# Two stages of a two-layer block: fewer whole key tiles, maxima earlier and a scaling on another engine in the second attention; transposes of gathered rows in halves between the expert products

## The chip, the cores and the metric

The kernel is one launch on one core of a Trainium2 chip. The metric is the device time of that launch in microseconds (us); 4358.14 us is the median of three runs of the kernel before. The engines named here are TensorE (PE; PEld is its weight load), VectorE (DVE), ScalarE (ACT), GpSimd (POOL) and SyncE (SP, which issues most DMAs).

## The reference

Two transformer-like blocks run one after the other on 2048 rows of 1024 features, in float32. The first mixes latent attention and a state space model; it is not touched. The second block, cut to what matters:

```
qa, ka, va, qr, kr, vr, gr = split(hx @ w_in)          # 8 query heads, 2 key heads of 64
k = concat([ka_context, ka]); v = concat([va_context, va])   # 256 + 2048 = 2304 keys
attn = softmax(q @ k.T * 64**-0.5) @ v                 # bidirectional, every query sees every key
ret  = group_norm(retention(qr, kr, vr)) * gn_g + gn_b # 4 heads of 128: (o - mean) * rsqrt(var + eps)
x2 = x + gt1 * (concat([attn, ret * silu(gr)]) @ w_out)
h2 = modulate(rms_norm(x2))
# experts: one group of 4, then 2 of its 8 experts; 32 experts, each 1024 -> 512 -> 1024
y[token] += weight * ((silu(h2 @ w_gate[e]) * (h2 @ w_up[e])) @ w_down[e])
out = rms_norm(x2 + gt2 * y)
```

## The kernel before

Precision: most products are three fp32r products of split operands (`mm3`, L306: high by high, high by low, low by high). A split is a cast on ScalarE (`split`, L318) and a subtraction on VectorE (L319). A product with float32 operands takes two passes of the tensor engine, which the trace shows as two MATMUL records.

**Order.** The functions are Python code that traces instructions in program order. A planner then makes, when the program is built, one fixed list for each engine: when an engine is free in its plan, it takes from the instructions whose inputs and buffers are ready in the plan the one that stands first in program order. On the chip each engine goes through its list in order, and waits where an input or a buffer is later than planned. Tiles come from pools; a tag has a number of buffers (`bufs`), and a new tile of that tag waits until the oldest one's last reader is done.

**Second attention (`Attention2`, from L1097).** Sixteen blocks of 128 queries by two key heads make 32 units. In a unit, `run` (L1265) goes over 18 key tiles, t = 0 to 17, of 128 keys. For each t: `scores` makes two fp32r products (L1185, L1186) into a PSUM tile `ps`; `exps` takes the exponential on ScalarE (L1194, or L1192); five tiles behind, `values` multiplies the exponentials with the values. There are two kinds of key tile. For a *whole* tile (`WHOLE2`, L1093: 2, 4, 7, 9, 12, 14, 17) the exponential stays float32 and one float32 product is made (L1228, two passes; the ones in its weights give the sum of the exponentials). For a *split* tile the exponential is cast to a high part `ph` (L1196, ScalarE), the rest `pl` is subtracted on VectorE (`rest`, L1205), the high part is added to a sum `acc` on GpSimd (L1212), and two fp32r products are made (L1232, L1233).

While unit n runs, `top` (L1157) finds the maxima that unit n + 1 subtracts: twenty steps of a product `pa` (L1167, two PSUM buffers) and a maximum over its columns on VectorE (`nm`, L1168), one step for the maximum `mx` over these (L1171), and one step with four transposes of `mx` and the copy of its negative into `qm` on ScalarE (L1176). `TOP` (L1107) says how many of these 22 steps are called after key tile t; what is left is done at t = 0 of the next unit, before its first scores, whose second product needs `qm`.

At t = 1, 9, 11 and 15 (`SIDE`) one step of the retention is called (`Retention.steps`). Its second loop has six steps for each of 16 chunks: transposes of queries and keys; transposes of scaled queries and the next state `rst` (L1049); scores; output `on` copied to SBUF with its mean and variance (L1070, L1072) and the inverse root `r4` (L70 on VectorE, then a power on GpSimd, L72); the scaling of `on` on VectorE, one instruction for each of four heads (L1076); and transposes of `on` with the group norm's gain on ScalarE (`ot`, L1084). The transposes here and those of `mx` share one PSUM buffer.

**Experts (`phase_moe`, L2345).** 32 experts in order of their row counts. The 15 largest have two blocks of 128 rows, the others one (a loop at the end takes what is left over); `turns` (L2075) sets them in turn, one of one block, one of two. For each expert three weight matrices of 2 MB come in four chunks each; each chunk is split into `whi` (ScalarE, L2250) and `wlo` (VectorE, or GpSimd for every sixth, L2253). There are 5 buffers for raw chunks and 12 for split ones, so the splits run about a matrix or two ahead of the products.

`rows` (L2258) gathers 128 rows of `h2` by an indirect DMA on GpSimd's queue into `xg` (two buffers), and transposes them in two halves of four 128 x 128 transposes into a PSUM tile `pt` (two buffers), each split into `xh` and `xl`. `gate` and `up` (through `into`, L2274) multiply in four chunks of six matmuls for each block of rows. `turned` (L2303) transposes the hidden tile `hg` through the same two `pt` buffers and splits it into `hh` and `hl`. `down` (L2316) gathers the rows of `x2` into `xo`, makes two products `py` of twelve matmuls for each block, scales, adds, normalizes and scatters the rows back.

One turn of the loop (L2372) has this program order, for the expert at hand (xs), the next one (xs2) and the one after (xs3): shares of xs2; gate weights and gate of xs2; `turned` of xs; up weights and up of xs2; `begin` of xs3, which reads its number on SP, gathers its rows, transposes and splits all of them; down weights and down of xs.

Of the kernel before, what the change touches and what calls it, by code (L numbers as in the profile page):

```python
# [10 lines left out]
F = mybir.dt.float32  # L11
# [869 lines left out]
HR = 4  # L881
# [71 lines left out]
class Retention:  # L953
# [16 lines left out]
    def steps(self, wk, bank):  # L970
# [55 lines left out]
        for n in range(NT):  # L1026
# [46 lines left out]
            k.rsqrt(r4, mv[:, :, 1], 1)  # L1073
            yield
            for h in range(HR):
                nc.vector.tensor_scalar(on[:, h], on[:, h], mv[:, h, 0:1], r4[:, h:h + 1], op0=OP.subtract, op1=OP.mult)  # L1076
# [16 lines left out]
WHOLE2 = (2, 4, 7, 9, 12, 14, 17)  # L1093
# [3 lines left out]
class Attention2:  # L1097
# [7 lines left out]
    TOP = (1, 1, 1, 2, 1, 1, 2, 1, 2, 1, 1, 1, 1, 1, 1, 1, 1, 1)  # L1105
# [1121 lines left out]
class Experts:  # L2227
# [30 lines left out]
    def rows(self, tx, lx):  # L2258

        k, nc, wk = self.k, self.k.nc, self.wk  # L2260
        xg = wk.tile([128, D], F, name="xg")
        nc.gpsimd.indirect_dma_start(out=xg, out_offset=None, in_=k.h2,
                                     in_offset=bass.IndirectOffsetOnAxis(ap=tx, axis=0))
        xh, xl = (wk.tile([128, 8, 128], R, name="x" + n, bufs=self.xs) for n in "hl")
        for half in range(2):
            pt = self.ps.tile([128, 4, 128], F, name="pt")
            for q in range(4):
                k.tr(pt[:, q], xg[:, (4 * half + q) * 128:(4 * half + q + 1) * 128])
            split(nc, xh[:, 4 * half:4 * half + 4], xl[:, 4 * half:4 * half + 4], pt)
        return tx, lx, xh, xl  # L2270

    def into(self, name, xs, w):
# [17 lines left out]
    def up(self, xs, hs, w):  # L2290
        for hg, z in zip(hs, self.into("pu", xs, w)):
            self.k.nc.vector.tensor_tensor(hg, hg, z, op=OP.mult)
# [23 lines left out]
    def down(self, xs, ts, w, gt, tbs):  # L2316
# [28 lines left out]
def phase_moe(k):  # L2345
# [6 lines left out]
    with ExitStack() as ctx:  # L2352
        x = Experts(k, ctx, 5, 12, 4, 3)

        def begin(r):
            e = nc.sync.value_load(k.ids[0:1, r:r + 1], min_val=0, max_val=NE - 1)
            return e, [x.rows(k.txs[:, b, r:r + 1], k.lxs[:, b, r:r + 1]) for b in range(2 if r < N2 else 1)]
# [4 lines left out]
        e, xs = begin(seq[0])  # L2362
# [7 lines left out]
        with k.tc.issue_after(x.mm.ins):  # L2370
            e2, xs2 = begin(seq[1])
# [16 lines left out]
def phase_end(k):  # L2388

    nc = k.nc  # L2390
    with ExitStack() as ctx:
# [3 lines left out]
        with k.tc.For_i(0, n, 1) as i:  # L2395
# [24 lines left out]
            rows = [x.rows(*places(k, wk, ix))]  # L2420
# [64 lines left out]
```

## Time and profile before

| | |
|---|---|
| runs | 4355.51, 4358.14 (median), 4358.15 us |
| profiled execution | 4347.35 us, span of its instructions 4345.5 us |
| granted clock, mean over the span | 0.961 |
| TensorE, VectorE busy over the span | 4035.4 us (93%), 2956.5 us (68%) |
| ScalarE, GpSimd busy over the span | 2153.2 us (50%), 1766.6 us (41%) |
| second attention | 2111 to 3079 us |
| experts | from about 3355 us to the end |

Busy times are sums over the whole span; the two stages have their own. A matmul's record is longer than the time it keeps the engine, since matmuls overlap: the distance from one start to the next tells what it costs. In rows of the order of time, the bracket is the idle time of the engine before the instruction and what ended it. The granted clock is the share of TensorE's full clock that was granted; its two levels are 1.2 and 2.4 GHz.

### The profile page before, as it was taken

The numbers are of one execution on the slowest core, as the hardware profiler recorded it, in microseconds if no ns is written. First come the engines' busy times: TensorE is split into PE (matmuls) and PEld (weight loads), VectorE is DVE, ScalarE is ACT, GpSimd is POOL, SyncE is SP. The second block draws the span as 40 slices with busy tenths as digits, with TensorE's granted clock in tenths as the row PEclk, the third lists the DMA queues.
The fourth block names the chain that finished last, engine by engine and source line by source line (L and its number), as shares of the span: only waits on it lengthen the run. The fifth ranks groups of instructions, "written<-read, shape, count | busy, mean of one in ns | idle before, by whom it ended". The sixth has DMA issues, their size and how long they took to land. (4 is left out here: it accounts for less than half of the span.)

```text
span 4345.5 us, 59078 instructions
## 1 busy us (share of the span) xinstructions
PE 4035.4 (93%) x19522; PEld 3202.2 (74%) x19522; DVE 2956.5 (68%) x5239; ACT 2153.2 (50%) x3910; POOL 1766.6 (41%) x2209
## 2 busy tenths in 40 slices
PE   7999879999998899999999999999997899999996
PEld 5777768888886778788666666666686677777775
DVE  7564258888644447544588788777565788888885
ACT  3233355555543334332366666666421666665664
POOL 3340058885001532222365555555200444444442
PEclk9999989999999999999999999999998999999998
DMA  5543772232225445333531211211533788887884
GB/s 141 164 152 119 232 240 75 92 104 81 69 75 171 137 148 183 119 117 102 145 111 53 60 47 51 56 38 33 154 133 118 284 285 292 289 285 279 278 283 155
DMA packets 436483, 646.66 MB, mean 149 GB/s; under 512 B 92193, under 2 KB 232737, under 8 KB 435917
## 3 DMA queue, kind: packets, MB, share of 16 engines
q1 hardware_dynamic: 407356, 561.75, 40.5%
q0 software_dynamic: 21840, 66.25, 4.1%
q10 hardware_dynamic: 6976, 14.85, 1.1%
q8 instruction: 155, 2.54, 0.2%
q14 instruction: 156, 1.27, 0.1%
HBM read 495.88 MB, written 155.64 MB: 150 GB/s over the span
## 5 line engine op out<-in xcount | busy, mean ns | idle before, releaser
L2253 DVE TENSOR_TENSOR wlo<-raw,whi 128x1024 fp32r<-128x1024 f32 x320 | 500.8, 1578 | 60.6 <-ACT whi L2250 55.0
L1168 DVE TENSOR_REDUCE nm<-pa 128x1 f32<-128x512 f32 (+1 forms) x640 | 391.7, 630 | 134.3 <-PE pa L1167 131.1
L2250 ACT CAST whi<-raw 128x1024 fp32r<-128x1024 f32 x384 | 387.2, 1051 | 147.1 <-PE pu L310 61.1
L1212 POOL TENSOR_TENSOR acc<-acc,ph 128x512 f32<-128x512 f32 x288 | 368.8, 1281 | 192.3 <-ACT ph L1196 187.6
L1167 PE MATMUL pa<-kk,q 128*128 128x512 f32 (+1 forms) x640 | 307.9, 490 | 28.6 <-DVE nm L1168 22.8
L310 PE MATMUL z<-wh,hlo 128*128 128x512 f32 (+2 forms) x816 | 305.7, 375 | 0.0
L308 PE MATMUL z<-wh,hhi 128*128 128x512 f32 (+2 forms) x768 | 291.2, 381 | 6.5 <-DVE zo L455 2.4
L1194 ACT ACTIVATE ps<-ps 128x512 f32<-128x512 f32 x352 | 204.5, 586 | 179.6 <-PE ps L1186 149.0
L309 PE MATMUL z<-wl,hhi 128*128 128x512 f32 (+2 forms) x768 | 290.2, 378 | 2.5 <-DVE wl L319 2.5
L1205 DVE TENSOR_TENSOR pl<-ps,ph 128x512 fp32r<-128x512 f32 x352 | 238.5, 683 | 43.9 <-ACT ph L1196 40.8
L72 POOL TENSOR_TENSOR nr<-nr,mhalf 128x1 f32<-128x1 f32 x98 | 61.3, 627 | 500.7 <-DVE nr L70 440.9
L1185 PE MATMUL ps<-q,kk 128*128 128x512 f32 x576 | 250.5, 435 | 0.1
L661 PE MATMUL s<-kn,q 128*128 128x512 f32 x768 | 229.8, 407 | 9.3 <-ACT p L674 5.5
L1186 PE MATMUL ps<-qm,kl 65*128 65x512 f32 x576 | 233.6, 407 | 0.2 <-ACT qm L1176 0.2
L1228 PE MATMUL o<-p,vw 128*128 128x512 f32 x448 | 229.1, 592 | 0.0
L693 ACT CAST ph<-pt 128x512 fp32r<-128x512 f32 x256 | 143.0, 597 | 152.1 <-PE pt L65 148.9
L739 PE MATMUL o<-ph,v 128*128 128x256 f32 x1024 | 215.6, 292 | 0.2 <-ACT ph L693 0.2
L697 DVE TENSOR_TENSOR pl<-pt,ph 128x512 fp32r<-128x512 f32 x256 | 168.0, 685 | 67.1 <-ACT ph L693 66.5
L1196 ACT CAST ph<-ps 128x512 fp32r<-128x512 f32 x352 | 202.7, 589 | 17.3 <-ACT ps L1194 0.4
L1167 PEld LDWEIGHTS pa<-kk,q 128*128 128x128 f32 x640 | 124.2, 194 | 110.8 <-DVE nm L1168 58.4
L2253 POOL TENSOR_TENSOR wlo<-raw,whi 128x1024 fp32r<-128x1024 f32 x64 | 159.8, 2496 | 95.6 <-ACT whi L2250 94.3
L661 PEld LDWEIGHTS s<-kn,q 128*128 128x128 f32 x768 | 141.5, 191 | 53.8 <-ACT p L674 6.4
(631 smaller groups left out, 11685.6 us busy)
## 6 DMA issues: line engine op xcount, KB each, us to landing
raw<-in_moe_w_gate SPq DMA_DIRECT2D x128, 512.0 KB
raw<-in_moe_w_up SPq DMA_DIRECT2D x128, 512.0 KB
raw<-in_moe_w_down SPq DMA_DIRECT2D x128, 512.0 KB
raw<-in_w_in SPq DMA_DIRECT2D x136, 256.0 KB
w<-in_w_ada SPq DMA_DIRECT2D x96, 256.0 KB
xt<-in_x SPq DMA_DIRECT2D x32, 512.0 KB
xt<-x SPq DMA_DIRECT2D x28, 512.0 KB
rv<-rv SPq DMA_DIRECT2D x34, 256.0 KB
```

Of the source, the lines that this page charges most:

```text
L308: nc.tensor.matmul(out, lh, rh, start=start, stop=False)
L309: nc.tensor.matmul(out, lh, rl, start=False, stop=False)
L310: return nc.tensor.matmul(out, ll, rh, start=False, stop=stop)
L661: self.nc.tensor.matmul(sp[:, c - c0:e - c0], l, r, start=n == 0, stop=n == len(ops) - 1)
L1167: nc.tensor.matmul(pa[:, :c1 - c0], q[:, h], kk[:, c0:c1], start=True, stop=True)
L1168: nc.vector.tensor_reduce(nm[:, h, c:c + 1], pa[:, :c1 - c0], axis=AX.X, op=OP.max)
L1185: nc.tensor.matmul(ps, kk[:, ts], q, start=True, stop=False)
L1186: nc.tensor.matmul(ps, kl[:, ts], qm, start=False, stop=True)
L1205: nc.vector.tensor_tensor(lo, ps, hi.bitcast(F), op=OP.subtract)
L1212: nc.gpsimd.tensor_tensor(acc, u["acc"], hi.bitcast(F), op=OP.add)
L2250: nc.scalar.copy(hi, raw)
L2253: i = eng.tensor_tensor(lo, raw, hi.bitcast(F), op=OP.subtract)
```

## The change

In the second attention: (1) four key tiles are whole, 3, 8, 13 and 17, where there were seven; the other fourteen are split. (2) `TOP` has other counts. (3) The scaling of `on` by mean and inverse root is an activation on ScalarE with scale `r4` and bias `m4`, where `m4` = -mean * r4 is made by one new VectorE instruction for all four heads, in the same step as the root.

```diff
             k.rsqrt(r4, mv[:, :, 1], 1)
+            m4 = wk.tile([128, HR], F, name="m4")
+            nc.vector.scalar_tensor_tensor(m4, mv[:, :, 0], -1.0, r4, op0=OP.mult, op1=OP.mult)
             yield
             for h in range(HR):
-                nc.vector.tensor_scalar(on[:, h], on[:, h], mv[:, h, 0:1], r4[:, h:h + 1], op0=OP.subtract, op1=OP.mult)
+                nc.scalar.activation(on[:, h], on[:, h], AF.Identity, scale=r4[:, h:h + 1], bias=m4[:, h:h + 1])
...
-WHOLE2 = (2, 4, 7, 9, 12, 14, 17)
+WHOLE2 = (3, 8, 13, 17)
...
-    TOP = (1, 1, 1, 2, 1, 1, 2, 1, 2, 1, 1, 1, 1, 1, 1, 1, 1, 1)
+    TOP = (1, 2, 1, 2, 1, 1, 2, 1, 1, 2, 1, 1, 2, 1, 1, 1, 0, 1)
```

In the experts: `rows` takes all blocks of an expert, issues their gathers, and returns a generator of steps; a step is one half of one block (four transposes and the split), in the order first half of each block, then second half of each. `begin` of xs3 stands ahead of `turned`. `up` of xs2 takes a step before its chunks 1 and 3, `down` of xs one after each of its products `py`, and what is left is done after `down`. So four steps of a two-block expert lie two in up and two in down, and the two steps of a one-block expert both in up. The first two experts and the loop at the end do all steps at once.

```diff
-    def rows(self, tx, lx):
+    def rows(self, ixs):
         k, nc, wk = self.k, self.k.nc, self.wk
-        xg = wk.tile([128, D], F, name="xg")
-        nc.gpsimd.indirect_dma_start(out=xg, out_offset=None, in_=k.h2,
-                                     in_offset=bass.IndirectOffsetOnAxis(ap=tx, axis=0))
-        xh, xl = (wk.tile([128, 8, 128], R, name="x" + n, bufs=self.xs) for n in "hl")
-        for half in range(2):
-            pt = self.ps.tile([128, 4, 128], F, name="pt")
-            for q in range(4):
-                k.tr(pt[:, q], xg[:, (4 * half + q) * 128:(4 * half + q + 1) * 128])
-            split(nc, xh[:, 4 * half:4 * half + 4], xl[:, 4 * half:4 * half + 4], pt)
-        return tx, lx, xh, xl
+        xs, gs = [], []
+        for tx, lx in ixs:
+            gs.append(wk.tile([128, D], F, name="xg"))
+            nc.gpsimd.indirect_dma_start(out=gs[-1], out_offset=None, in_=k.h2,
+                                         in_offset=bass.IndirectOffsetOnAxis(ap=tx, axis=0))
+            xs.append((tx, lx, *(wk.tile([128, 8, 128], R, name="x" + n, bufs=self.xs) for n in "hl")))
+
+        def steps():
+            for h in (slice(0, 4), slice(4, 8)):
+                for xg, (_, _, xh, xl) in zip(gs, xs):
+                    pt = self.ps.tile([128, 4, 128], F, name="pt")
+                    for q in range(4):
+                        k.tr(pt[:, q], xg[:, (h.start + q) * 128:(h.start + q + 1) * 128])
+                    split(nc, xh[:, h], xl[:, h], pt)
+                    yield
+        return xs, steps()
...
         for c in range(4):
+            if c % 2:
+                next(steps, None)
...
                     mm3(nc, py, hh[:, q], hl[:, q], w[q][0][:, ns], w[q][1][:, ns], q == 0, q == 3)
+                next(steps, None)
...
+            steps = iter(())
+            if n + 1 < NE:
+                e3, xs3, steps = begin(seq[n + 1])
             ts = x.turned(hs)
             if n < NE:
-                x.up(xs2, hs2, x.weights(e2, 1))
-            if n + 1 < NE:
-                e3, xs3 = begin(seq[n + 1])
-            x.down(xs, ts, x.weights(e, 2), k.gt2, tbs)
+                x.up(xs2, hs2, x.weights(e2, 1), steps)
+            x.down(xs, ts, x.weights(e, 2), k.gt2, tbs, steps)
+            for _ in steps:
+                pass
```

## Rows read from the trace of the kernel before

**Rows 1.** Busy us (instructions) by engine, granted clock, DMA share, GB/s by stage.
```profile
core 0: us, PE busy (x) PEld busy (x) DVE busy (x) ACT busy (x) POOL busy (x), PEclk, DMA share, GB/s
2703.20:2729.00 25.80, 25.43 (x105) 17.90 (x106) 20.92 (x41) 19.62 (x39) 16.03 (x14) 1.00 0.19 50
...
2111.00:3079.00 968.00, 926.70 (x3859) 648.28 (x3858) 761.50 (x1465) 633.25 (x1187) 559.56 (x452) 0.98 0.23 61
...
3420.00:4290.00 870.00, 814.54 (x3656) 664.20 (x3657) 744.68 (x778) 535.47 (x657) 401.14 (x274) 0.96 0.81 282
```
**Rows 2.** Waits in the second attention: us in total, times, longest.
```profile
POOL acc L1212 <- ACT ph L1196: 286.0, 174, 6.7
PE pa L1167 <- DVE nm L1168: 22.8, 17, 3.4
PE pt L65 <- DVE mx L1171: 10.9, 11, 2.9
DVE on L1076 <- POOL r L72: 6.4, 16, 1.3
```
**Rows 3.** TensorE in order of time: start, duration, line, count, idle before.
```profile
2750.13 0.39 PE L1233 MATMUL o<-pl,v 128*128 128x512 f32 x1
2750.36 0.28 PE L1167 MATMUL pa<-kk,q 128*128 128x256 f32 x1
...
2750.94 1.02 PE L1228 MATMUL o<-p,vw 128*128 128x512 f32 x2
2751.40 0.80 PE L1167 MATMUL pa<-kk,q 128*128 128x512 f32 x1
2752.03 0.39 PE L1185 MATMUL ps<-q,kk 128*128 128x512 f32 x1
...
2758.20 0.79 PE L1167 MATMUL pa<-kk,q 128*128 128x512 f32 x1 [3.41 <-DVE nm L1168]
```
**Rows 4.** Busy us and granted clock in the four us behind that wait.
```profile
2758.00:2762.00 4.00, 3.80 (x12) 3.05 (x13) 3.37 (x7) 1.29 (x3) 0.73 (x1) 0.57 0.00 0
```
**Rows 5.** VectorE and GpSimd in order of time, during that wait.
```profile
2754.41 3.13 DVE L1076 TENSOR_SCALAR on<-on,mv,r 128x128 f32<-128x128 f32 x4 [1.27 <-POOL r L72]
2754.36 2.59 POOL L1212 TENSOR_TENSOR acc<-acc,ph 128x512 f32<-128x512 f32 x2
```
**Rows 6.** Line 1076: count, duration in ns, least, median and greatest.
```profile
L1076 DVE TENSOR_SCALAR on<-on,mv,r x64: 331/343/2514, 2301.0 to 2979.2; 128x128 f32<-128x128 f32 x64
```
**Rows 7.** TensorE's waits in the experts, 3420 to 4290 us: the first.
```profile
PE pt L65 <- DVE xl L319: 48.3, 14, 3.5
```
**Rows 8.** TensorE in order of time around one of them.
```profile
3726.18 1.03 PE L65 MATMUL pt<-ident,hg 128*128 128x128 f32 x8
3726.97 0.48 PE L308 MATMUL pu<-whi,xh 128*128 128x512 f32 x1
...
3732.78 1.25 PE L65 MATMUL pt<-ident,xg 128*128 128x128 f32 x8
...
3739.39 0.66 PE L65 MATMUL pt<-ident,xg 128*128 128x128 f32 x4 [3.49 <-DVE xl L319]
```
**Rows 9.** ScalarE and VectorE in order of time there.
```profile
3730.76 1.06 ACT L318 CAST hh<-pt 128x512 fp32r<-128x512 f32 x2
3732.04 1.28 DVE L319 TENSOR_TENSOR hl<-pt,hh 128x512 fp32r<-128x512 f32 x2
3733.74 3.25 DVE L2253 TENSOR_TENSOR wlo<-raw,whi 128x1024 fp32r<-128x1024 f32 x1 [0.43 <-ACT whi L2250]
3738.66 1.27 DVE L319 TENSOR_TENSOR xl<-pt,xh 128x512 fp32r<-128x512 f32 x2
```
**Rows 10.** Groups of instructions in the attention: busy us, mean ns; idle before.
```profile
L1212 POOL TENSOR_TENSOR acc<-acc,ph 128x512 f32<-128x512 f32 x288 | 368.8, 1281 | 192.3 <-ACT ph L1196 187.6
L1205 DVE TENSOR_TENSOR pl<-ps,ph 128x512 fp32r<-128x512 f32 x352 | 238.5, 683 | 43.9 <-ACT ph L1196 40.8
L1196 ACT CAST ph<-ps 128x512 fp32r<-128x512 f32 x352 | 202.7, 589 | 17.3 <-ACT ps L1194 0.4
L1084 ACT ACTIVATE ot<-pt,decays 128x128 f32<-128x128 f32 x64 | 24.1, 457 | 11.7 <-PE pt L65 11.7
```

More of the change, by code (lines that the diff above doesn't have):

```diff
@@ L2256, in weights, with into @@
         return out
-    def rows(self, tx, lx):
+    def rows(self, ixs):
         k, nc, wk = self.k, self.k.nc, self.wk
-        xg = wk.tile([128, D], F, name="xg")
-        nc.gpsimd.indirect_dma_start(out=xg, out_offset=None, in_=k.h2,
-                                     in_offset=bass.IndirectOffsetOnAxis(ap=tx, axis=0))
-        xh, xl = (wk.tile([128, 8, 128], R, name="x" + n, bufs=self.xs) for n in "hl")
-        for half in range(2):
-            pt = self.ps.tile([128, 4, 128], F, name="pt")
-            for q in range(4):
-                k.tr(pt[:, q], xg[:, (4 * half + q) * 128:(4 * half + q + 1) * 128])
-            split(nc, xh[:, 4 * half:4 * half + 4], xl[:, 4 * half:4 * half + 4], pt)
-        return tx, lx, xh, xl
-    def into(self, name, xs, w):
+        xs, gs = [], []
[13 more added lines that the diff above has]
+        return xs, steps()
+    def into(self, name, xs, w, steps=iter(())):
         pz = [self.ps.tile([128, DE], F, name=name) for _ in xs]
         for c in range(4):
+            if c % 2:
+                next(steps, None)
             for z, (_, _, xh, xl) in zip(pz, xs):
@@ L2288, in gate, with up @@
         return hs
-    def up(self, xs, hs, w):
-        for hg, z in zip(hs, self.into("pu", xs, w)):
+    def up(self, xs, hs, w, steps=iter(())):
+        for hg, z in zip(hs, self.into("pu", xs, w, steps)):
             self.k.nc.vector.tensor_tensor(hg, hg, z, op=OP.mult)
@@ L2314, in turned, with down @@
         return ts
-    def down(self, xs, ts, w, gt, tbs):
+    def down(self, xs, ts, w, gt, tbs, steps=iter(())):
         k, nc, wk = self.k, self.k.nc, self.wk
@@ L2356, in begin @@
             e = nc.sync.value_load(k.ids[0:1, r:r + 1], min_val=0, max_val=NE - 1)
-            return e, [x.rows(k.txs[:, b, r:r + 1], k.lxs[:, b, r:r + 1]) for b in range(2 if r < N2 else 1)]
+            return e, *x.rows([(k.txs[:, b, r:r + 1], k.lxs[:, b, r:r + 1]) for b in range(2 if r < N2 else 1)])
         seq = turns()
-        e, xs = begin(seq[0])
+        e, xs, steps = begin(seq[0])
+        for _ in steps:
+            pass
         hs = x.gate(xs, x.weights(e, 0))
@@ L2370, in phase_moe @@
         with k.tc.issue_after(x.mm.ins):
-            e2, xs2 = begin(seq[1])
+            e2, xs2, steps = begin(seq[1])
+            for _ in steps:
+                pass
         for n in range(1, NE + 1):
@@ L2375, in phase_moe @@
                 hs2 = x.gate(xs2, x.weights(e2, 0))
+            steps = iter(())
+            if n + 1 < NE:
+                e3, xs3, steps = begin(seq[n + 1])
             ts = x.turned(hs)
             if n < NE:
-                x.up(xs2, hs2, x.weights(e2, 1))
-            if n + 1 < NE:
-                e3, xs3 = begin(seq[n + 1])
-            x.down(xs, ts, x.weights(e, 2), k.gt2, tbs)
+                x.up(xs2, hs2, x.weights(e2, 1), steps)
+            x.down(xs, ts, x.weights(e, 2), k.gt2, tbs, steps)
+            for _ in steps:
+                pass
             if n < NE:
@@ L2419, in phase_end @@
             nc.vector.tensor_copy(ix, lf[:, 0:1])
-            rows = [x.rows(*places(k, wk, ix))]
+            rows, steps = x.rows([places(k, wk, ix)])
+            for _ in steps:
+                pass
             hs = x.gate(rows, x.weights(e, 0))
```

## The prediction

> **What bounds the kernel now.** I read the busy time by stage first, then the waits of TensorE in the two stages that the change touches, then the order of time around the longest of them. The chain that ended last is of no use here: the page gives only its last few instructions.
>
> The table by stage shows the second attention between 2111 and 3079 us, with TensorE busy 926.7 of 968 us, VectorE 761.5, ScalarE 633.3 and GpSimd 559.6; and 870 us of the experts, with TensorE at 814.5, VectorE 744.7 and ScalarE 535.5, and the DMA engines at 0.81 [rows 1]. TensorE is the bound of both. What is not busy in it, 41 and 55 us, is short stops in a stream that otherwise runs on. So two things can move the time: less streaming, and fewer stops.
>
> In attention the stops are named: 22.8 us in 17 waits for a maximum (`nm`), and 10.9 us in 11 waits for the last maximum (`mx`) [rows 2]. The longest for `nm` ends at 2758.20, after 3.41 us [rows 3], and in the four us behind 2758 the granted clock is 0.57, so much of it at 1.2 instead of 2.4 GHz [rows 4]. What VectorE did meanwhile is one group: the four scalings `on` at 2754.41, which waited 1.27 us for GpSimd's root and then took 3.13 us beside two of GpSimd's adds [rows 5], though the median of one is 0.343 us and only the maximum 2.514 [rows 6].
>
> In the experts there is one stop: 14 waits, the longest 3.5 us, 48.3 us together, of a transpose for `xl` [rows 7]. At 3732.78 eight transposes of gathered rows fill both `pt` buffers; the next four need the first buffer back and start 3.49 us late, at 3739.39 [rows 8], because `xl` came only at 3738.66, behind a `wlo` of 3.25 us [rows 9]. This comes once per pair of experts, one with one block of rows and one with two.
>
> **The change part by part.**
>
> *Four whole key tiles for seven.* Three tiles in each of 32 units, 96 in all, go from one product in two fp32 passes to two fp32r products. From 2750.94 to 2752.03 lie the two passes and one 512-column product, 1.09 us; one 512-column product alone takes 2750.36 - 2750.13 = 0.23; so a whole tile takes 0.86 and a split one 2 x 0.23 = 0.46 [rows 3]. Saved: 96 x 0.40 = 38 us of streaming, all on the path. Added: 96 casts on ScalarE (0.589 each, 57 us), 96 subtractions on VectorE (0.683, 66 us) and 96 adds on GpSimd (1.281, 123 us) [rows 10]. They lie beside TensorE as long as VectorE keeps up: in the unit from 2703.2 it has 20.92 us of 25.8; with three subtractions that is 23.0, against 25.4 - 1.2 = 24.2 for TensorE [rows 1]. With only two `pa` buffers between the two that is close, so the ends are 0 (VectorE sets the pace) and 38; I take 23, six tenths. Where the values are made, three more key tiles get a cast and a small subtraction for a copy, once each: nothing.
>
> *Scaling on ScalarE.* 64 VectorE instructions go, sixteen groups of four. ScalarE gets 64 activations like those of `ot`, 0.457 us each, 29 us [rows 10]; with the casts it has 633 + 57 + 29 = 719 of some 920 us, and its spare time covers them. If a scaling waits there, the exponentials behind it wait too, and TensorE for those. What goes from the path is the 22.8 us of waits for `nm` and the slow clock behind them: in the four us after 2758 TensorE starts 12 matmuls where 4 / 0.23 = 17 fit [rows 4], 1.2 us lost; if ten of the 17 waits cost as much, 12 us, together 35. The ends are 0 and 35; I take 22, because the added subtractions will make new short waits. Against it stands the new VectorE instruction `m4`. It waits for the root as `on` did, 6.4 us in 16 waits, the longest 1.3 [rows 2], and behind it on VectorE stand the maxima and subtractions for which TensorE waits. No row shows it; its cost lies between 0 and 16 x 1.3 = 21 us. I take 6, the wait of the same place before. Net 16.
>
> The Trainium skill speaks against this part (page "SBUF — State Buffer", section "Who interferes with whom"): a VectorE instruction with two SBUF inputs and a GpSimd instruction that reads SBUF share a read port, and the later one is blocked for the whole of the other. The trace agrees in kind: 0.343 us became 2.514 for `on` [rows 6]. By this rule `m4`, with two SBUF operands, can lose one add, 1.28 us, sixteen times, 20 us, and the sum below would be 14 us smaller; the subtractions `pl`, with one operand in PSUM, would lose nothing.
>
> *Maxima early.* The generator of the next unit's maxima has 22 steps. The old schedule calls 21 within a unit and leaves the transposes of `mx` to the first moment of the next; the new one calls all 22, the last product at key tile 14, `mx` at 15, the transposes at 17. This goes at the 10.9 us of waits for `mx` [rows 2]. What is late next is `qm`, on ScalarE behind the exponential of tile 17. Ends 0 and 11; I take 6.
>
> Attention together: 23 + 16 + 6 = 45 us.
>
> *Experts.* No matmul, transpose or split is added or removed; they move. The gathers of the rows and the register load on SP are issued ahead of the hidden tile's transposes and the up weights: past the up loads on SP's queue and past GpSimd's share of the up splits. Of TensorE's waits in this stage none named in the view is for a gather, and the `xg` buffer that a gather waits for comes free earlier too, as its transposes do: I cost this at nothing; each us by which a gather came late would be one of TensorE. For a two-block expert the four groups of four transposes now stand before chunks 1 and 3 of the one-block up product and after the first two down products. With two buffers each is wanted again 30 matmuls later (18 of up and 12 of down), 6.9 us, against some 5.5 us that it stayed taken here (3733.8 to 3739.3), so I let the wait for `xl` go. But the first group stands only 6 matmuls behind the hidden tile's transposes, which hold both `pt` buffers. Up starts at 3726.97, so chunk 1 at 3728.4. The buffer comes back with the first `hl`, about 3732.7, since the cast `hh` ran on ScalarE only at 3730.76 [rows 8, 9]. Where the group stands right there in TensorE's order, TensorE stops for 4.3 us; where the planner, which knows that the buffer is taken, lets more up products pass first, for less, down to 0. I take the middle, 2.1. Saved per pair: 3.5 - 2.1 = 1.4, times 14: 20 us. Ends: -0.8 x 14 = -11 (a loss) and +48.
>
> *Sum.* 45 + 20 = 65 us. The profiled execution took 4347.4 us (span 4345.5); it would take 4282. The median of the runs, 4358.1, lies 10.8 above it; I take the same 65 off: 4293 us.
>
> **Rivals.**
>
> *The stop only changes its place in the experts.* For: hidden tile and gathered rows use the same two buffers, and 5.5 us pass from the former's transposes to the first `hl`. Against: the planner has 24 up matmuls to put in between. Attention as forecast, experts at -6, the middle of 0 and -11: 4358 - 45 + 6 = 4319.
>
> *All stops go and all streaming counts.* For: every other engine has spare time by stage. Against: each engine's order is fixed, and a stop here lets the others catch up for the next place. 38 + 35 + 11 and 48: 4226.
>
> *VectorE sets the pace of attention.* For: 23.0 against 24.2 us in the plain unit. Against: `on` leaves it. Streaming and scaling gain nothing, maxima 5, experts 20: 4333.
>
> *GpSimd falls behind; slower.* The root for `m4` queues behind adds while VectorE stands in front of the maxima. Six adds ahead are 7.7 us. At 2758.20 VectorE had been away for 1.27 + 3.13 = 4.4 us and TensorE stopped for 3.4, so TensorE pays 1.0 less, 6.7, and 1.2 of slow clock: 7.9 x 16 = 126. Off go 38 + 35 + 6 and the experts' 20, 99: +27, so 4385. It decides from the fifth add (99 / 16 = 6.2 us a time). For: 123 us more adds, 683 of some 920 us. Against: GpSimd waits for ScalarE's `ph` 286 us in this stage [rows 2], so such a queue should be rare.
>
> **How the numbers follow.** Forecast 0.42 (its own range 4265 to 4320), stop only moved 0.18, all gained 0.13, VectorE's pace 0.13, GpSimd behind 0.14. The range for 8 in 10, 4232 to 4352, holds the first two, VectorE's pace with the bounds of its unknowns, and half of "all gained"; it leaves out the other half and most of the slower case. A measurement of this kernel tells about 0.2%, 9 us, from no change. Faster: 0.42 + 0.18 + 0.13 + 0.08 of VectorE's pace = 0.81; its other 0.05 and 0.02 of the last case are no change, 0.07; slower 0.12.
>
> **What the changed profile would show.** Right: no long wait of a transpose for `xl`, and at most some 2 us per pair for `hl`; the attention about 920 us long, no wait of over 2 us for `nm` and no half clock in it; next to no wait for `mx`. Wrong: a wait for `hl` of 4 us or more per pair (experts); VectorE over 95% busy in plain units (streaming); `m4` waiting several us for its root (scaling); `qm` in the place of `mx` (maxima).

## The result, and the profile after

The changed kernel takes 4381.41 us (median of 7 runs, 4365.85 to 4388.31) where the kernel before takes 4355.51 (7 runs beside them, 4341.55 to 4359.03): ratio 1.0063, 95% interval 1.0046 to 1.0080. It is 26 us slower; 4293 was forecast, and the range ended at 4352. Its profiled execution took 4383.1 us, 36 more than that of before. Of these, 11 lie ahead of the second attention, in code that the change doesn't touch, 12 in the attention (from its first scores at 2123.2 to its last at 3097.4, 974 us for 962) and 13 behind it, where the experts are. One execution tells these only roughly: in the seven kernels of this document whose code up to the end of the attention is that of before, it begins between 2111 and 2121 and takes 959 to 969 us.

Busy time by stage of the changed kernel, to hold against [rows 1] (us, then TensorE, weight loads, VectorE, ScalarE, GpSimd with instructions, granted clock, DMA share, GB/s):

```profile
2722.00:2749.70 27.70, 26.14 (x114) 18.95 (x114) 23.99 (x52) 22.16 (x45) 18.36 (x15) 1.00 0.28 72
2123.00:3098.00 975.00, 903.90 (x3844) 653.62 (x3843) 788.47 (x1508) 700.08 (x1345) 676.64 (x546) 0.96 0.23 61
3430.00:4300.00 870.00, 793.84 (x3607) 644.11 (x3606) 703.75 (x765) 528.79 (x648) 382.22 (x269) 0.97 0.81 281
```

TensorE is busy 23 us less in the attention, and the stage is longer all the same: 71 us of it are idle instead of 41, and the granted clock is 0.96 instead of 0.98. The plain unit went from 25.8 to 27.7 us with VectorE at 24.0, 87%. The waits of the stage, against [rows 2] (us in total, times, longest):

```profile
DVE m L1075 <- POOL r L72: 32.9, 16, 3.2
PE pa L1169 <- DVE nm L1170: 29.2, 17, 3.3
PE pa L1169 <- DMA q<-q: 16.7, 18, 2.8
```

No wait for `mx` is left. The waits for `nm` are all there, 17 again and 29.2 us for 22.8, and the wait for the root has grown from 6.4 to 32.9 us: 3.1 to 3.2 us in eight of the 16 times, 0.9 to 1.1 in the others. Three times as long as before is a wait for a load, in which the first product of a unit's maxima waits for the queries `q`: 16.7 us. In the kernel before it was the third of TensorE's waits in this stage:

```profile
PE pa L1167 <- DMA q<-q: 5.4, 11, 1.4
```

One of the long stops for `nm` in order of time (start, duration, in brackets the idle time and what ended it), and the stretch behind it:

```profile
2773.67 2.63 POOL L1214 TENSOR_TENSOR acc<-acc,ph 128x512 f32<-128x512 f32 x2 [0.20 <-ACT ph L1198]
2776.25 1.02 POOL L72 TENSOR_TENSOR r<-r,mhalf 128x4 f32<-128x4 f32 x1
2777.31 1.21 DVE L1075 SCALAR_TENSOR_TENSOR m<-mv,r 128x4 f32<-128x4 f32 x1 [3.15 <-POOL r L72]
2778.55 1.65 ACT L1078 ACTIVATE on<-on,m,r 128x128 f32<-128x128 f32 x4 [4.55 <-DVE m L1075]
2779.17 0.50 PE L1169 MATMUL pa<-kk,q 128*128 128x512 f32 x1 [3.30 <-DVE nm L1170]
...
2779.00:2783.00 4.00, 3.83 (x12) 3.07 (x13) 3.36 (x7) 3.18 (x8) 0.49 (x1) 0.58 0.15 33
```

The root stands behind two adds on GpSimd, VectorE stands 3.15 us at `m4` (the trace calls it `m`), then needs 1.21 us for 128x4 elements, TensorE stops 3.30 us, and the granted clock of the next four us is 0.58, much of it at 1.2 GHz, as in [rows 4]. In [rows 5] VectorE was away as long, 4.4 us, but 1.3 of it were the wait and 3.1 the scaling; now 3.15 are the wait. Such a stop of 3.3 us comes eight times here, every 90 us; in the kernel before one was as long, and two others were 2.9 and 3.0.

In the experts, the waits of 3430 to 4300 us, and below the last dots two of the kernel before that stand behind [rows 7] in 3420 to 4290:

```profile
PE py L308 <- DVE xo L2346: 38.7, 13, 4.8
PE pt L65 <- DVE hl L319: 35.3, 14, 9.4
...
DVE xo L2346 <- DMA xo<-out,tx: 33.1, 14, 3.9
...
PE py L308 <- DVE xo L2334: 3.9, 1, 3.9
DVE xo L2334 <- DMA xo<-out,tx: 3.5, 7, 0.8
```

The stop for `xl` is gone. Two others are there in each pair of experts: one for `hl`, which was forecast, and one that was not, of the third down product, which needs a `py` buffer back. One pair in order of time, against [rows 8, 9]:

```profile
3697.12 1.04 POOL L2353 DMA_INDIRECT out<-yo,tb  x1 [4.09 <-DVE yo L2352]
3697.49 0.66 PE L65 MATMUL pt<-ident,xg 128*128 128x128 f32 x4 [1.58 <-DVE hl L319]
3702.55 1.74 POOL L2334 DMA_INDIRECT xo<-out,tx  x1 [1.94 <-DMA out<-yo,tb]
3709.38 0.69 DVE L2346 TENSOR_TENSOR xo<-py,xo 128x512 f32<-128x512 f32 x1 [2.35 <-DMA xo<-out,tx]
3710.22 0.47 PE L308 MATMUL py<-whi,hh 128*128 128x512 f32 x1 [3.30 <-DVE xo L2346]
```

`py` comes free with the add of `xo`; the add waits for the gather of `xo`; the gather starts at 3702.55, when the scatter of the expert before (3697.12) has landed.

### The profile page after: what moved, and what is told of

It reads as the page before. It is cut to its first block, busy times and chain, and to the rows that moved or that the text cites. A ratio compares the mean times of both kernels' runs of the same rounds, so it can differ in the third digit from the quotient of the medians.

```text
span 4381.3 us, 59694 instructions
## 1 busy us (share of the span) xinstructions
PE 4013.6 (92%) x19522; PEld 3202.8 (73%) x19522; DVE 2960.2 (68%) x5290; ACT 2221.9 (51%) x4070; POOL 1868.2 (43%) x2305
## 5 line engine op out<-in xcount | busy, mean ns | idle before, releaser
L1214 POOL TENSOR_TENSOR acc<-acc,ph 128x512 f32<-128x512 f32 x384 | 493.3, 1285 | 195.7 <-ACT ph L1198 182.3
L2255 DVE TENSOR_TENSOR wlo<-raw,whi 128x1024 fp32r<-128x1024 f32 x320 | 464.6, 1463 | 96.5 <-ACT whi L2252 91.4
L1207 DVE TENSOR_TENSOR pl<-ps,ph 128x512 fp32r<-128x512 f32 x448 | 303.6, 681 | 44.6 <-ACT ph L1198 42.2
L1196 ACT ACTIVATE ps<-ps 128x512 f32<-128x512 f32 x448 | 255.6, 586 | 137.9 <-PE ps L1188 101.3
L1169 PE MATMUL pa<-kk,q 128*128 128x512 f32 (+1 forms) x640 | 267.4, 438 | 48.0 <-DVE nm L1170 29.2
L1187 PE MATMUL ps<-q,kk 128*128 128x512 f32 x576 | 280.5, 490 | 11.5 <-DVE pl L1207 8.9
L1198 ACT CAST ph<-ps 128x512 fp32r<-128x512 f32 x448 | 255.3, 592 | 19.0 <-issue 2.1
L308 PE MATMUL py<-whi,hh 128*128 128x512 f32 x376 | 159.0, 423 | 50.0 <-DVE xo L2346 47.8
L1235 PE MATMUL o<-pl,v 128*128 128x512 f32 x448 | 182.2, 408 | 8.2 <-ACT os L1247 8.2
```

The lines of the kernel that those rows point to most:

```text
L308: nc.tensor.matmul(out, lh, rh, start=start, stop=False)
L1169: nc.tensor.matmul(pa[:, :c1 - c0], q[:, h], kk[:, c0:c1], start=True, stop=True)
L1187: nc.tensor.matmul(ps, kk[:, ts], q, start=True, stop=False)
L1196: self.nc.scalar.activation(ps, ps, AF.Exp, scale=self.scale)
L1198: self.nc.scalar.copy(hi, ps)
L1207: nc.vector.tensor_tensor(lo, ps, hi.bitcast(F), op=OP.subtract)
```

## The experiments

Times are medians in us, with that of the kernel before run beside it.

| run | this | before | ratio, 95% interval |
|---|---|---|---|
| e1_experts | 4362.2 | 4346.1 | 1.0036 (1.0024 to 1.0048) |
| e2_scaling | 4332.0 | 4346.1 | 0.9967 (0.9956 to 0.9978) |
| e3_whole4 | 4362.4 | 4346.1 | 1.0032 (1.0020 to 1.0044) |
| e4_maxima | 4354.0 | 4346.1 | 1.0021 (1.0010 to 1.0032) |
| e5_whole4_q3 | 4351.2 | 4353.7 | 0.9994 (0.9980 to 1.0008) |
| e6_scaling_q3 | 4347.2 | 4353.7 | 0.9987 (0.9975 to 0.9998) |
| e7_scaling_whole4_q3 | 4329.0 | 4353.7 | 0.9938 (0.9920 to 0.9955) |
| e8_experts_py | 4351.3 | 4353.7 | 0.9993 (0.9980 to 1.0006) |
| e9_scaling_whole4_qfar | 4323.0 | 4346.4 | 0.9945 (0.9923 to 0.9966) |
| e10_experts_pool_add | 4429.9 | 4346.4 | 1.0182 (1.0158 to 1.0206) |
| e11_all_qfar | 4317.5 | 4346.4 | 0.9930 (0.9908 to 0.9952) |
| e12_m4_pool | 4318.6 | 4346.4 | 0.9929 (0.9907 to 0.9952) |
| e13_experts_free_gather | 4292.2 | 4350.8 | 0.9864 (0.9849 to 0.9879) |
| e14_before_free_gather | 4276.9 | 4350.8 | 0.9838 (0.9819 to 0.9858) |
| e15_attn_best | 4308.3 | 4350.8 | 0.9902 (0.9887 to 0.9917) |
| e16_after_qfar | 4333.6 | 4350.8 | 0.9964 (0.9952 to 0.9976) |
| e17_steps_in_down | 4418.9 | 4350.1 | 1.0153 (1.0136 to 1.0169) |
| e18_best | 4337.3 | 4350.1 | 0.9966 (0.9951 to 0.9981) |

### Each part alone

e1 is the second diff of the change without the first; the other three are one part of the first:

```diff
e2: +            nc.vector.scalar_tensor_tensor(m4, mv[:, :, 0], -1.0, r4, op0=OP.mult, op1=OP.mult)
e2: +                nc.scalar.activation(on[:, h], on[:, h], AF.Identity, scale=r4[:, h:h + 1], bias=m4[:, h:h + 1])
e3: +WHOLE2 = (3, 8, 13, 17)
e4: +    TOP = (1, 2, 1, 2, 1, 1, 2, 1, 1, 2, 1, 1, 2, 1, 1, 1, 0, 1)
```

> The kernel before with the change of the experts alone; the attention is as before. Theory (two new stops outweigh the old one): the stop of a transpose for xl (48 us in 14 waits) is gone, but about fifteen stops for hl of 1.5 to 2.9 us (37 us together) and fifteen stops of the third down product for its py buffer of 1.2 to 4.8 us (48 us together), whose VectorE add waits for the gather of xo, take its place: 10 us slower than before, 6 to 15. Rival 1 (the 10 us between the two profiled executions are spread from run to run): within 5 us of before. Rival 2 (the step as predicted, spoilt only by the attention's change): 20 us faster.

> The kernel before with the scaling of on as activations on ScalarE and the new VectorE instruction m4, nothing else. Theory (m4 is harmless by itself and waits long for its root only because GpSimd got 96 more adds): m4 waits 6 to 12 us in 16 times, the 3.3 us stop for nm shrinks below 2 us, and the time falls by 8 to 16 us. Rival (the wait for the root is inherent in the order of VectorE, whatever GpSimd's load): m4 waits 25 us or more, longest over 2.5, TensorE keeps one stop of about 3 us for nm per unit with retention, and the time is within 5 us of before or above it.

> The kernel before with four whole key tiles for seven, nothing else. Theory (VectorE sets the pace once three more subtractions per unit are in): TensorE is busy some 20 us less in the attention, plain units go from 25.5 to 27 us and more, with more short stops for nm; the time rises by 10 to 20 us. Rival (the shorter stream counts, as predicted, and only the combination with m4 spoils it): the time falls by 15 to 25 us, plain units are 25 us or less.

> The kernel before with the new counts of the maxima's steps alone (all 22 within the unit). Theory: the 10.9 us of waits for mx go, nothing else comes in with VectorE at its old load: 4 to 10 us faster. Rival (steps called two at a time put two maxima one behind the other on VectorE, and two pa buffers don't cover that): the waits for nm grow by as much as mx gives, within 4 us of before or slower.

Experts +16, scaling -14, four whole tiles +16, maxima +8: together +26, what the whole change measures; each is known to about 5 us, so the match to the microsecond is luck. In e2 the theory held, and its marks can be read: `m4` waits little, the stops for `nm` are nearly gone, and a smaller one for `pl` is in their place (waits in the attention):

```profile
PE ps L1187 <- DVE pl L1207: 14.4, 8, 2.1
PE pa L1169 <- DVE nm L1170: 1.2, 5, 0.3
...
DVE m L1075 <- POOL r L72: 10.8, 16, 0.8
```

So the wait of 3.2 us at `m4` isn't in the new order of VectorE as such. e3's theory held in time, but the wait that grew most is not VectorE's `nm` (31.3 us for 22.8): it is that for a load, `q`, 24.2 us against 5.4 in the kernel before. e4's theory fell. It lost as its rival said, but not for the rival's reason: `nm` rose by 2.2 us only, `q` to 11.4, while 10.9 us of `mx` went; what makes up the rest of its 8 us stays open. First the waits of e3, then the end of a unit there in order of time:

```profile
PE pa L1167 <- DVE nm L1168: 31.3, 16, 4.1
PE pa L1167 <- DMA q<-q: 24.2, 24, 2.3
...
2623.47 0.40 PE L1186 MATMUL ps<-qm,kl 65*128 65x512 f32 x1
2623.77 0.54 SPq L1152 DMA_DIRECT2D q<-q  x1
2628.24 0.73 PE L1167 MATMUL pa<-kk,q 128*128 128x512 f32 x2 [1.67 <-DMA q<-q]
```

There are two buffers of `q`. The load of the next unit's queries takes that of the unit before, which is free after its last scores (2623.47); the first product that needs them stands soon after, behind the first scores of the new unit. From issue to product it is 4.5 us here, with two other loads issued just ahead (2622.57 and 2623.20). In the kernel before it is 3.0:

```profile
2639.28 0.40 PE L1186 MATMUL ps<-qm,kl 65*128 65x512 f32 x1
2639.47 0.38 SPq L1152 DMA_DIRECT2D q<-q  x1
...
2642.47 0.50 PE L1167 MATMUL pa<-kk,q 128*128 128x512 f32 x1 [0.32 <-DMA q<-q]
```

In the kernel before, the old unit's last products, the transposes of `mx` and the new scores fill all but 0.32 of these three us.

### The queries a unit earlier

```diff
-        q = self.qp.tile([128, 4, 128], R, name="q")
+        q = self.qp.tile([128, 4, 128], R, name="q", bufs=3)      # qm the same
-                    if n + 1 < N:
-                        self.q[n + 1] = self.load_q(n + 1)
+                    if n + 2 < N:
+                        self.q[n + 2] = self.load_q(n + 2)
```

e9, e11, e12, e15, e16 and e18 ("qfar") keep one of the three buffers in that pool and two in the pool `wk`, and load the second unit's queries after the first keys.

> Four whole tiles as in e3_whole4, and three buffers instead of two for the queries q and qm, loaded one unit earlier. Theory (a good part of the loss of e3_whole4 is the first product of a unit's maxima, which waits for the load of q, 24.2 us in 24 waits, because the load starts only when the last scores of the unit before have been made): those waits are under 3 us, the time is 15 to 22 us below e3_whole4, about that of the kernel before. Rival (VectorE sets the pace of the unit; a wait removed here comes back as waits for nm or pl): the waits for q go, but the time falls by less than 6 us.

> The scaling on ScalarE as in e2_scaling, seven whole tiles, with the same three buffers for q and qm. Theory: the 6.3 us of waits for q go and little else: 3 to 7 us below e2_scaling, 17 to 21 below the kernel before. Rival (the moved loads delay other loads on SP, or the waits come back elsewhere): within 3 us of e2_scaling.

> Scaling on ScalarE, four whole tiles and three buffers for q and qm; old counts of the maxima's steps, old experts. Theory (with q early and VectorE freed of the scaling, what is left of the loss of four whole tiles is that GpSimd, with 96 more adds, makes the root late and m4 stands in VectorE for it): m4 waits 25 us or more for its root, the waits for nm stay at 20 us or more, and the time lies 0 to 10 us above e6_scaling_q3. Rival (the shorter stream counts once q is early): 10 to 25 us below e6_scaling_q3.

> As e7_scaling_whole4_q3, but the third buffer of q and qm lies in another pool, and the second unit's queries are loaded behind the first keys. Theory (the single stop of 11.6 us of the first product of all in e7, which is not in e2_scaling, is due to the larger pool, which overlaps buffers of the stage before, so that the first loads start 37 us later, at 2108 instead of 2071): that stop goes and with it 8 to 12 us: 33 to 37 us below the kernel before. Rival (the loads of the first keys are short of something else): the stop stays, within 4 us of e7.

> As e9_scaling_whole4_qfar with the new counts of the maxima's steps too: the whole change of the attention with q early; experts as before. Theory (the loss of 8 us in e4_maxima is the wait for q, 11.4 instead of 5.4 us, and more of it where the unit is shorter): with q early the counts gain the waits for mx (11.3 us in e7): 3 to 10 us below e9. Rival (the counts put two maxima one behind the other and move the root among GpSimd's adds; m4 waits 32.9 us in the changed kernel and 17.1 in e7): m4 waits 25 us or more, the stops for nm rise above 25 us, 5 to 15 us above e9.

Against the kernel before, four whole tiles go from +16 (e3) to -2.5 (e5), which can't be told from none. With the scaling, e7 lies 18 us below e6: the shorter stream counts, the rival of e7's expectation. The larger pool of e5 to e7 has a price, one stop of the first product of all, 11.6 us in e7, as the first load of `q` is issued at 2108 (2068 in the kernel before). It may be why e6 gained less than e2 (-7 against -14, outside both its theory and its rival): in the profiles e6's attention is no longer than e2's, 949 us for 952, but begins at 2130 instead of 2104. In e9 this stop is gone (one of 5.5 us for `q` is there), but the gain against e7 can't be told from none: -23 and -25 against the kernel before. In e11, with the new counts of the maxima too, no wait for `mx` is left (11.6 us in e9) and the time is 5 us below e9; e9's runs lie between 4314 and 4333, so this alone isn't clear of noise.

### The wait for the root

```diff
+            nc.vector.tensor_scalar(m4, mv[:, :, 0], -1.0, None, op0=OP.mult)
             k.rsqrt(r4, mv[:, :, 1], 1)
+            nc.gpsimd.tensor_tensor(m4, m4, r4, op=OP.mult)
```

> As e9_scaling_whole4_qfar, but VectorE negates the mean before the root, and GpSimd multiplies it by the root behind its power, so that no VectorE instruction waits for GpSimd. Theory (the 20.3 us of stops for nm in e7 come from VectorE standing at m4 for the root): they fall below 8 us and the time by 8 to 18 us against e9. Rival (the stops for nm come from the retention's other VectorE work, bn_stats, bn_aggr and rst beside GpSimd's adds): nm stays at 15 us or more, within 4 us of e9.

> The whole change of the attention with q early (e11_all_qfar) and m4's product on GpSimd (e12_m4_pool), experts as before. Theory (what is left of the stops for nm, 22 us in e11, is VectorE at m4, 12.1 us): nm under 12 us, 4 to 12 us below e11. Rival (ScalarE now waits for GpSimd instead, with the exponentials behind it, as p and qm did in e12, 25 us together): within 4 us of e11 or above it.

In e12 no VectorE instruction waits for GpSimd, and the waits for `nm` fall from 21.2 (e9) to 6.1 us; ScalarE's take part of their place (waits of e12):

```profile
PE ps L1191 <- ACT qm L1181: 12.9, 10, 1.6
PE ps L1190 <- ACT p L1197: 12.5, 11, 1.8
PE pa L1172 <- DVE nm L1173: 6.1, 11, 2.9
```

The gain, 4 us over e9, is less than the 8 expected and within the spread of e9's runs. e15, with the new counts as well, is the best version of all, 42.5 us below the kernel before, where e11 is 29 and e12 28 below: each of the two steps gains some 14 us when the other is there. Its attention takes 916.5 us at a granted clock of 0.99.

### The changed kernel with the queries early

> The changed kernel with all its parts, and q and qm in three buffers, loaded a unit earlier as in e9. Theory (the late load of q turned the attention's change from a gain of some 29 us into a loss of about 10): 35 to 45 us below the changed kernel, 8 to 20 below the kernel before. Rival (the 16.7 us of waits for q in the changed kernel are all that it costs): 10 to 20 us below the changed kernel, not below the kernel before.

e16 has every part of the change, and its edit differs from it in the load alone. It is 17 us faster than the kernel before where the change is 26 slower, as its theory had it: the late load, with all that hung on it, cost 43 us. Its attention, and its waits there:

```profile
2112.50:3038.40 925.90, 887.01 (x3840) 638.87 (x3838) 798.88 (x1510) 698.87 (x1343) 676.50 (x543) 0.98 0.24 64
...
PE pa L1171 <- DVE nm L1172: 22.3, 31, 1.6
PE pa L1171 <- DMA q<-q: 5.0, 1, 5.0
...
DVE m L1075 <- POOL r L72: 12.1, 16, 1.1
```

The stage is 49 us shorter than in the changed kernel: 32 of idle TensorE and 17 of busy. Of the 32, `q` itself gives 12. The rest are other waits that went with it: the longest for `nm` is 1.6 instead of 3.3 us, the one for the root 1.1 instead of 3.2, and the clock is 0.98 instead of 0.96, 2% of 926 us, about the 17 us of busy time. At the clock of before TensorE is now busy 34 us less than there (887 us for 921, from the first to the last scores), near the 38 of the shorter stream. With the load's time in its plan the planner wrote other lists: the root starts 0.1 us after its input in all 16 cases here, and in the changed kernel two adds, 2.6 us, stand between in eight of them. That this order, and not something else, shortened the root's wait was not tried by itself.

### The experts

```diff
e8:  -  nc.vector.scalar_tensor_tensor(py, py, tb[:, 0:1], gt[:, ns], op0=OP.mult, op1=OP.mult)
e8:  -  nc.vector.tensor_tensor(xo[:, ns], py, xo[:, ns], op=OP.add)
e8:  +  nc.vector.scalar_tensor_tensor(yo[:, ns], py, tb[:, 0:1], gt[:, ns], op0=OP.mult, op1=OP.mult)
e8:  +  nc.vector.tensor_tensor(xo[:, ns], yo[:, ns], xo[:, ns], op=OP.add)     # e10: nc.gpsimd
e13, e14: -  nc.gpsimd.indirect_dma_start(out=xo, out_offset=None, in_=k.x2, ...
e13, e14: +  nc.gpsimd.indirect_dma_start(out=xo, out_offset=None, in_=k.h2, ...
e17: -  x.up(xs2, hs2, x.weights(e2, 1), steps)
e17: +  x.up(xs2, hs2, x.weights(e2, 1))
```

> The change of the experts alone, as e1_experts, but the first of the two VectorE instructions behind a down product writes its result to yo in SBUF instead of back to py, and the add of xo reads it there, so that py comes free without the gather of xo. Theory (the new stop of the third down product is the wait of its py buffer for an add that waits for the gather): the 48 us of stops for xo go, hl's 37 us stay, the time is 25 to 45 us below e1_experts, 10 to 30 below the kernel before. Rival 1 (the chain from the scatter to the next gather and its add sets the period, wherever TensorE waits for it): the stop moves to another place of the pair and the time is within 8 us of e1_experts. Rival 2 (the weights' DMA sets the period once TensorE no longer stops): at most 15 us below e1_experts, with waits for raw chunks or whi and wlo on TensorE.

> The change of the experts alone with py emptied into yo as in e8_experts_py, and the add of yo and xo on GpSimd instead of VectorE. Theory (in e8 the wait for the gather of xo was not gone but stood in VectorE, in front of hl, whose stop of TensorE had grown from 37 to 59 us): with no VectorE instruction waiting for the gather, the stop for hl falls to about 2 us a pair (30 us), py costs under 10, and the time is 10 to 30 us below e8. Rival (the chain from scatter to gather sets the period; GpSimd's adds of 1.3 us lengthen it): the waits come back at the normalization and the next gather, within 8 us of e8 or above it.

> The change of the experts alone, with the rows for xo gathered from h2 instead of x2, so that no gather waits for the scatter of the expert before (the sums of this kernel are of other rows; the amount of work is the same). Theory (the chain scatter, landing, gather, add sets the period once the stop for xl is gone): the 48 us of stops of py for xo fall below 10, hl's stop of about 2 us a pair stays, the time is 30 to 50 us below e1_experts. Rival (the gather is late for its own length, 8 us among the weights' traffic, or for its place in GpSimd's queue): within 10 us of e1_experts.

> The kernel before, with the rows for xo gathered from h2 instead of x2, as in e13. Theory (before, the stop for xl covered the chain: it is there whether or not the gather waits): the 48 us of stops for xl stay at 40 or more and the time is within 6 us of the kernel before, so that e13 is the faster of the two by 15 to 35 us. Rival (the chain costs the kernel before too, and what e13 gains has nothing to do with the transposes): 20 us or more below the kernel before, with no gain of e13 over it.

> The change of the experts alone, with no step in the up product: all groups of transposes stand behind the products of down. Theory (what the part loses is the stop for hl, 37 us in e1 and 36 in e13, because the first group stands right behind the hidden tile's transposes): hl's stops fall under 8 us, the time is 12 to 25 us below e1_experts, within 8 us of the kernel before or below it; stops of py for xo of 30 to 50 us stay. Rival (the stop only wanders: with the groups in down, py and the next gate wait for xl and xo as long): the stops of TensorE sum to 80 us or more as in e1, the time is within 6 us of e1.

> The attention of e15_attn_best with the experts of e17_steps_in_down and py emptied into yo as in e8_experts_py. Theory (the gains add): 0 to 25 us below e15, that is 4285 to 4310 where the kernel before takes 4350. Rival (in the experts the chain from scatter to gather sets the period, 75 us of it by e13, and moved transposes only choose who waits for it): within 5 us of e15 or up to 15 us above it.

In e1 the theory held, with 16 us for the 6 to 15 expected: TensorE's waits for `xl` (48 us) are gone, and 42.3 us for `py` and 26.9 for `hl` have come. e8 takes back what e1 lost (-2 for +16 against the kernel before), less than the 25 to 45 us expected: the wait for the gather stands in VectorE as in e1 (36.6 us in 14 times, 35.4 in e1), and the stop for `hl` is 59.3 us. What ties the longer stop to that wait is not shown; the two lie some 20 us apart, as in e1. e10's theory fell outright, and its rival, that the adds lengthen the chain, held by sign: with the add on GpSimd the kernel is 84 us slower, and TensorE waits 125 us for `hl`.

e13 and e14 gather other rows for `xo`, and so don't compute the block; they show only what the order of scatter and gather costs. e13 gains more than the 30 to 50 us expected, and e14's theory fell: I held that the kernel before hid the gather behind the stop for `xl`. Without the dependence it gains 74 us, as the rival said, and with the moved transposes the gain is 75 (e13 against e1, each against its kernel before). The part costs as much without the dependence (e13 less e14, 15 us) as with it (16), though by other stops: there only 18 us of `xl` can go, and `hl` comes with 36. Waits of TensorE and 820 us of the stage in e14, then the waits in e13:

```profile
PE pt L65 <- DVE xl L319: 17.8, 15, 3.5
3380.00:4200.00 820.00, 795.72 (x3697) 649.42 (x3696) 690.45 (x790) 540.95 (x662) 415.86 (x279) 0.99 0.88 305
```
```profile
PE pt L65 <- DVE hl L319: 36.4, 14, 9.8
PE py L308 <- DVE xo L2344: 11.2, 9, 1.3
```

In e14 the stop for `xl` fell from 48 to 18 us and the clock rose from 0.96 [rows 1] to 0.99, 3% of 820 us or 25. Its stops for `xl`, 3.1 to 3.5 us in all 14 pairs before, are about 1 us in 11 of 15. What stands in GpSimd's queue beside VectorE is one reason that the rows show. In the kernel before (first) and in e14 (second):

```profile
3790.21 1.04 POOL L2341 DMA_INDIRECT out<-yo,tb  x1 [3.52 <-DVE yo L2340]
3791.28 2.41 POOL L2253 TENSOR_TENSOR wlo<-raw,whi 128x1024 fp32r<-128x1024 f32 x1
3791.53 3.24 DVE L2253 TENSOR_TENSOR wlo<-raw,whi 128x1024 fp32r<-128x1024 f32 x1 [0.43 <-ACT whi L2250]
```
```profile
3825.14 1.04 POOL L2341 DMA_INDIRECT out<-yo,tb  x1 [3.07 <-DVE yo L2340]
3826.48 0.99 POOL L2323 DMA_INDIRECT xo<-h,tx  x1 [0.30 <-ACT whi L2250]
3826.56 1.22 DVE L2253 TENSOR_TENSOR wlo<-raw,whi 128x1024 fp32r<-128x1024 f32 x1
3827.47 2.55 POOL L2253 TENSOR_TENSOR wlo<-raw,whi 128x1024 fp32r<-128x1024 f32 x1
```

While the scatter is on its way GpSimd splits weights beside VectorE, whose `wlo` ahead of `xl` takes 3.24 us instead of 1.22. The order on VectorE differs too: before, a second `wlo` stands ahead of `xl`, in e14 it comes behind. How much of the 74 us is this and how much the shorter chain, the two runs don't separate.

e17's theory fell: without the group in up there is no stop for `hl`, as expected, but the kernel is 69 us slower. The edit has a cost of its own, so it doesn't tell what the group's place in up costs (waits of TensorE and GpSimd, then GpSimd in order of time):

```profile
PE py L308 <- DVE xo L2344: 87.5, 13, 7.9
POOL xg L2265 <- PE pt L65: 126.7, 12, 11.3
...
3833.22 1.48 POOL L2332 DMA_INDIRECT xo<-out,tx  x1 [2.20 <-DMA out<-yo,tb]
3848.18 0.95 POOL L2265 DMA_INDIRECT xg<-h,tx  x1 [10.97 <-PE pt L65]
3849.13 0.59 POOL L72 TENSOR_TENSOR ss<-ss,mhalf 128x1 f32<-128x1 f32 x1
```

Down starts sooner and meets the late `xo` with nothing between; and the early gather of `xg`, whose buffer the later transposes still hold, stands 11 us in GpSimd's queue ahead of the root `ss` that the next scatter needs. e18 is 13 us below the kernel before, but about 30 worse than e15 (the two differences to the kernel before), twice what its rival allowed: the attention's gain, less what these experts lose.

## Why the prediction was wrong, point by point

The forecast was 65 us faster, the measurement is 26 slower. Of these 91 us the load of the queries is 43 (e16), and the experts are 36 (20 faster forecast, 16 slower in e1); with `q` early the attention still gains about 16 less than forecast (29 in e11 for 45).

**The step that failed in the attention** is that of the streaming and the maxima, by what it left out, and so put at nothing: both make the end of a unit shorter, and a load that starts there came late; four whole tiles alone raised its waits by 18.8 us (e3), the new counts alone by 6.0 (e4). The prediction asked which engine is late next, and `q` is no engine's work; that TensorE waited for it already, 5.4 us in 11 times, was not read. With `q` early and the scaling on ScalarE the terms come out near what was taken. *Four whole tiles*: 23 taken, 18 measured (e6 to e7); with the scaling still on VectorE 2.5 in time (e5, less the price of its pool). *Maxima*: 6 taken, 5 measured (e9 to e11), not clear of noise. *Scaling*: 16 taken, 14 measured alone (e2); the wait at `m4` was 10.8 us for the 6 taken. In the changed kernel that term failed too: `m4` waited 32.9 us, up to 3.2 at a time, close to the sign of being wrong that was named, and the stops for `nm` stayed, 29.2 us; both shrank when the load was early (e16: 12.1 and 22.3). The attention was to be about 920 us long; it is 928 in e11 and 926 in e16 by their first and last scores, and 974 in the changed kernel.

**VectorE as the pace** is not what happened: in the changed kernel a plain unit has VectorE at 24.0 of 27.7 us, not over 95% busy. In e5, where the scaling stays on VectorE, the waits for `nm` are 32.4 us, and still the attention of its profile is shorter than before, 951 us for 962. **GpSimd behind** gave 4385, next to the 4381 measured, and that is luck: two adds stood ahead of the root in eight of 16 times, and never six; TensorE's stops for `nm` are 29.2 us in all, not 126 with the slow clock; and the scaling alone is a gain.

**The step that failed in the experts** is "so I let the wait for `xl` go", as a gain. `xl`'s stop did go, `hl` cost 35.3 / 14 = 2.5 us a pair for the 2.1 taken (1.8 without the first two pairs); but only the `pt` buffers were followed. The third down product needs one of two `py` buffers, and they come back with the gather of `xo`: 38.7 us of stops that the sum put at nothing. In the kernel before:

```profile
3802.68 0.68 DVE L2334 TENSOR_TENSOR xo<-py,xo 128x512 f32<-128x512 f32 x1
3805.51 0.39 PE L308 MATMUL py<-whi,hh 128*128 128x512 f32 x1
```

The add that frees the buffer ends at 3803.36, 2.1 us before the product: of a stop of 3.5 us no more than that could be won in this pair, if the add came no sooner. The gathers that the prediction costed at nothing were those of `xg`; that of `xo` it didn't look at, though the view of [rows 7] has a stop of `py` for `xo`, once, 3.9 us, and VectorE waited for that gather 3.5 us in 7 times (33.1 in 14 after). So "there is one stop" was read too quickly. One end stays open: without the dependence of the gather the part loses as much (e13 and e14), so the gather is what the changed kernel waits for, but not the only way in which this part loses.

On the port that VectorE and GpSimd share the Trainium skill (page "SBUF — State Buffer", section "Who interferes with whom") would have made `m4` lose one whole add, 20 us in all. The trace agrees where the two meet: `m4` takes 1.21 us in eight of 16 times, each within 0.1 us behind the start of a GpSimd instruction of 1.25 us (L1262) and until its end, and 0.16 us in the eight with none beside it. So it lost 8 x 1.05 = 8 us; what was mis-sized is how often they meet.

## What to carry to other kernels

Before you count a stop as saved, look for what became ready during it: loads that start at the end of a unit, gathers behind a scatter, the last reader of every buffer that the next work needs. The latest of these bounds what can be won, 2.1 of 3.5 us in the pair above. When a unit gets shorter, its loads have to start earlier: here one more buffer turned a loss of 26 us into a gain of 17. And measure the parts alone first: here their sum is the whole's within the noise, and the waits of the worst one named the load.

## What the runs showed of the hardware

A stop of TensorE costs more than itself. Behind the stop of 3.30 us above, the granted clock of four us is 0.58, behind the 3.41 us of [rows 3] 0.57; in the kernel before, it is 0.66 and 0.57 behind two of 2.35 and 2.36 us (they end at 2487.2 and 2577.5), and 1.00 behind one of 2.16 (2667.5). The granted clock of the attention is 0.96 in the changed kernel, with eight stops of 3.3 us, and 0.98 in e16, where none but the first wait for `q` is over 1.8.

GpSimd holds VectorE up. On 128x4 elements `m4` took 1.21 us in the eight times that a GpSimd instruction ran beside it and 0.16 in the eight others. On 128x1024, `wlo` took 3.24 us when GpSimd's had started 0.25 us earlier, and 1.22 when its own was the first by 0.9 us; in 820 us of the experts, 54 of VectorE's 277 `wlo` took over 2 us in the kernel before, all of them beside one on GpSimd, and 30 of 299 in e14.
